# Shared PSUM pools, six split-weight buffers, the sample's attention ahead of the last two prompt tiles, and a new order of emission in a two-layer hybrid encoder

## The chip, the core and the metric

The kernel runs on one NeuronCore of a Trainium2 chip. Its engines are TensorE (PE, with its weight loads as PEld), VectorE (DVE), ScalarE (ACT), GpSimd (POOL) and SyncE (SP, which issues the DMAs). The metric is the device time of one execution in microseconds; lower is better.

## The reference

Two layers over a chunk of 1024 prompt frames and 8 sample streams of 16 frames each, model width 1024, all in float32. Each layer has a mixer (attention over a window of 128 keys with a sink, beside pooling over 2, 4, 8 and 16 frames) and a feed-forward part with a convolution of width 3 and a gate:

```python
def trunk_layer(x, ...):
    xn = rms_norm(x, norm_mix)
    q, k, v, u = mixer_inputs(xn, pos, w_in, q_gain, k_gain)   # one projection, 1024 -> 512+128+128+512
    attn = window_attention_prompt(q, k, v, sinks)             # prompt: 8 q heads, 2 kv heads, chunks of 64
    # sample: keys and values of a cache of 128 positions ahead of the new 16
    pool, new_pool = pool_mixer(u, pool_prev, w_pool, pool_scale)
    x = x + jnp.concatenate([attn, pool], axis=-1) @ w_out
    f, new_conv = conv_ffn(rms_norm(x, norm_ffn), conv_prev, w_up, conv_w, conv_b, w_down)   # D_FF = 2816
    x = x + f
    return x, keys[:, -WINDOW:], vals[:, -WINDOW:], new_pool, new_conv
```

The outputs are both streams' frames, and the newest keys, values, pooling rows and convolution rows.

## The kernel before

**Tiles and numbers.** The 1152 rows (1024 prompt, 128 sample) are nine tiles of 128; tile 8 is the sample. Three tiles make a block b = 0, 1, 2. Float32 products are made from split operands: `hi` is the value rounded by ACT to the fp32r type, `lo` the rest from DVE, and `mm3` makes three matmuls (L173 to L175) of each product.

**The mixer's streams.** Per block there are units k0 to k2 (k, v and q columns; 12 units each), u0 to u2 (pooling input, 8 units), p0 to p2 (the pooling's own matmuls, 4) and o0 to o2 (output projection and the addition to X, 16 units: eight for each half of the columns). n1 to n3 are the norms ahead of a layer's mixer, m0 to m2 those ahead of the feed-forward part. A unit takes one weight piece of 256 KB: SP loads it to `raw`, `w_split` makes hi (ACT, L198) and lo (DVE, L199).

**Attention** is one chain of steps, L.0, L.1 and so on. For a prompt tile: preparation of q and k (`prep`), then for each of two head groups g: `score` (matmuls L606/L607; DVE adds the mask and takes the maximum, L610), `soft1` (exp on ACT, L622), `soft2` (DVE scales, L635), `pt` (transposes of P on TensorE, L645) and `pv` (L658). The next tile's preparation is interleaved. The sample's tile has its own steps (`sample`, among them 64-wide score matmuls per stream, L762/L763), run after tile 7.

**Order.** Every unit and step is a token with a key (a time) and predecessors. The table `PLAN` holds each stream's first key and step (`o0=(87.72, 2.71)`: o0.i has key 87.72 + 2.71 i), the attention's key per tile (`L`), and flags e_*, which put a copy on DVE (1) or ACT (0). `arrange` walks the tokens by key and emits each as soon as its predecessors are out and the counted resources allow; one of these, `mm`, is four PSUM banks: a k or o unit group holds three, a u group two. Tile's scheduler then orders the instructions of each engine anew within their dependences.

**PSUM** is one tile of eight banks, with banks assigned by hand: 0 to 3 from a list (`mm_take`, `mm_give`), 4 and 5 in turn for scores and PV (`s`), 6 and 7 in turn for transposes and the pooling's matmuls (`tr`). The up stage uses banks 0 to 5 as three pairs.

**Feed-forward.** `sums` makes two chains, s0 and s1, for the two halves of the rows, from the transposed norms m: seven roundings (ACT L325, DVE L326) and four sums (L334). Up runs 22 rounds i of seven products n (`PRODUCTS`, a scheme with seven products instead of eight); each unit is 24 matmuls of 288 columns, 12 for each half s. In round 0 the halves are units of their own; the first three of round 0's weights come as `upw` tokens. `up_post` adds the results into rows (L943) or copies them (L949); then follow convolution and gate, stored to `gd` in DRAM. Down runs over three chunks of eight gate blocks, tile by tile: `down_load` reads a tile's gates (SP, then ACT L1055 and DVE L1056), `down_prep` loads and splits one block of down weights (L1044 to L1046). Layer 1's mixer begins under the last down units of layer 0 (tokens d.t).

## Time and profile before

| what | us |
|---|---|
| median of three runs (lowest to highest) | 2417.01 (2414.57 to 2417.25) |
| the profiled execution, its time | 2412.6 |
| its span | 2410.8 |
| TensorE busy | 2280.5 |
| VectorE busy | 1596.4 |
| ScalarE busy | 959.7 |
| mean granted clock of TensorE | 0.969 of full |

Layer 0's mixer takes the span's first 395 us, its up stage the time to 931, its down stage goes to about 1255 with layer 1's first units beside its end; layer 1's up stage runs from about 1605 to 2122. An engine's line in the slices gives its busy share in tenths for each fortieth of the span; PEclk is the clock that TensorE was granted in that slice. A group's row gives the line, engine, operation, what it writes and reads, and its count; then the busy time and the mean ns of one; then the idle time ahead of the group and what ended it. A wait's row gives the waiting line, the line waited for, microseconds in total, times, and the longest. A row of the chain gives start, duration and what.

### The profile page before, as it was taken

To read this page: it belongs to the slowest core of one execution; us is meant where nothing else is said; L and a number is where in the kernel's file an instruction comes from. 1 tells how busy PE (TensorE), PEld (TensorE's weight loads), DVE (VectorE), ACT (ScalarE), POOL (GpSimd) and SP (SyncE) were. 2 spreads that over 40 slices of the span, in tenths; PEclk is the share of its full clock that TensorE was granted. 3 is DMA by queue.
4 is the path that set the end of the run, shared out by engine and by line. 5 is a ranking of instruction groups with operands and counts; after the bars stand their busy time and mean duration, and the time that the engine had idled before them with its cause. 6 is when DMAs were issued, how large, how long until landed. Compare 5 with 4: busy or idle time off the path is not lost.

```text
span 2410.8 us, 35976 instructions
## 1 busy us (share of the span) xinstructions
PE 2280.5 (95%) x13610; PEld 2025.8 (84%) x13610; DVE 1596.4 (66%) x2942; ACT 959.7 (40%) x1774; POOL 201.6 (8%) x411
## 2 busy tenths in 40 slices
PE   7989979899999998999998899788999999989999
PEld 7757757899999997888887687578999999978887
DVE  5766665988888887233356776478888888853332
ACT  4555554534334334121236565454333433421110
POOL 0000000111111110000000000001111111100000
PEclk9989988899999999999999999889999999999999
DMA  6233332222222226364442333422222222273643
GB/s 218 62 112 122 99 117 89 84 79 70 79 75 71 77 75 225 131 218 164 143 135 61 99 127 102 133 89 65 65 80 78 69 79 75 79 246 125 222 157 109
DMA packets 244495, 271.77 MB, mean 113 GB/s; under 512 B 17410, under 2 KB 188370, under 8 KB 244290
## 3 DMA queue, kind: packets, MB, share of 16 engines
q1 hardware_dynamic: 244322, 269.48, 34.9%
q8 instruction: 107, 1.75, 0.3%
q14 instruction: 66, 0.54, 0.1%
HBM read 203.69 MB, written 67.42 MB: 112 GB/s over the span
## 4 chain that ended last, share of the span: by engine, by line
PE 82%; DVE 7%; DMA 5%; ACT 3%; issue 2%; SPq 1%; POOL 0%; ACTq 0%; DVEq 0%
PE psum L173 25%; PE psum L174 25%; PE psum L175 25%; PE psum L658 2%; DMA raw<-in_w_out_dram 2%; DVE W L199 1%; PE psum L305 1%; DVE B L326 1%; DMA raw<-in_w_in_dram 1%; PE psum L645 1%; DMA B<-gd 1%; DMA raw<-in_w_down_dram 1%; DVE B L334 1%; PE psum L461 1%; ACT W L198 1%
## 5 line engine op out<-in xcount | busy, mean ns | idle before, releaser
L173 PE MATMUL psum<-B,W 128*128 128x288 f32 (+1 forms) x1896 | 572.2, 302 | 18.3 <-ACT B L325 12.3
L174 PE MATMUL psum<-B,W 128*128 128x288 f32 (+1 forms) x1896 | 569.9, 301 | 8.1 <-DVE B L326 8.1
L175 PE MATMUL psum<-B,W 128*128 128x288 f32 (+1 forms) x1896 | 568.2, 300 | 0.0
L173 PEld LDWEIGHTS psum<-B,W 128*128 128x128 f32 x1896 | 359.4, 190 | 22.6 <-ACT B L325 13.9
L173 PE MATMUL psum<-B,B 128*128 128x512 f32 (+2 forms) x914 | 357.0, 394 | 20.1 <-ACT B L1055 10.3
L174 PEld LDWEIGHTS psum<-B,W 128*128 128x128 f32 x1896 | 358.8, 189 | 11.2 <-DVE B L326 10.2
L175 PEld LDWEIGHTS psum<-B,W 128*128 128x128 f32 x1896 | 358.9, 189 | 0.9 <-DVE W L199 0.5
L174 PE MATMUL psum<-B,B 128*128 128x512 f32 (+2 forms) x914 | 357.2, 391 | 0.0
L175 PE MATMUL psum<-B,B 128*128 128x512 f32 (+2 forms) x914 | 355.9, 391 | 0.0
L992 DVE SCALAR_TENSOR_TENSOR B<-B,cvp,B 128x1168 f32<-128x1168 f32 x176 | 250.5, 1428 | 7.9 <-ACT B L990 7.7
L173 PEld LDWEIGHTS psum<-B,B 128*128 128x128 f32 x914 | 172.9, 190 | 59.8 <-ACT B L198 11.5
L1083 DVE TENSOR_TENSOR B<-psum,B 128x512 f32<-128x512 f32 x108 | 74.5, 690 | 199.0 <-PE psum L175 198.9
L174 PEld LDWEIGHTS psum<-B,B 128*128 128x128 f32 x914 | 173.5, 190 | 37.6 <-DVE B L199 0.5
L175 PEld LDWEIGHTS psum<-B,B 128*128 128x128 f32 x914 | 172.8, 189 | 37.7 <-issue 0.2
L173 PE MATMUL psum<-W,B 128*128 128x512 f32 (+1 forms) x510 | 190.4, 386 | 9.5 <-ACT B L463 5.0
L199 DVE TENSOR_TENSOR W<-raw,W 128x512 fp32r<-128x512 f32 x184 | 125.8, 689 | 103.4 <-ACT W L198 102.7
L174 PE MATMUL psum<-W,B 128*128 128x512 f32 (+1 forms) x510 | 192.9, 379 | 0.9 <-DVE W L199 0.9
L868 ACT CAST W<-Q 128x512 fp32r<-128x512 f32 x132 | 81.8, 621 | 280.3 <-PE psum L175 280.1
L175 PE MATMUL psum<-W,B 128*128 128x512 f32 (+1 forms) x510 | 191.9, 381 | 0.0
L198 ACT CAST W<-raw 128x512 fp32r<-128x512 f32 x184 | 113.2, 620 | 166.9 <-PE psum L175 58.5
L943 DVE TENSOR_TENSOR B<-psum,PT 128x160 f32<-128x160 f32 (+2 forms) x356 | 147.8, 447 | 27.2 <-PE psum L175 27.1
L943 DVE TENSOR_TENSOR PT<-psum,PT 128x576 f32<-128x576 f32 (+1 forms) x138 | 100.4, 730 | 84.6 <-PE psum L175 84.3
(188 smaller groups left out, 3953.2 us busy)
## 6 DMA issues: line engine op xcount, KB each, us to landing
raw<-in_w_up_dram SPq DMA_DIRECT2D x176, 256.0 KB
xd<-B SPq DMA_DIRECT2D x63, 512.0 KB
B<-xd SPq DMA_DIRECT2D x63, 512.0 KB
raw<-in_w_in_dram SPq DMA_DIRECT2D x120, 256.0 KB
gd<-B SPq DMA_DIRECT2D x44, 576.0 KB
raw<-in_w_down_dram SPq DMA_DIRECT2D x88, 256.0 KB
B<-gd SPq DMA_DIRECT2D x36, 512.0 KB
raw<-in_w_out_dram SPq DMA_DIRECT2D x48, 256.0 KB
```

What stands on the lines that cost most here:

```text
L173: pe.matmul(out=out, lhsT=a[0], rhs=b[0], start=first, stop=False)
L174: pe.matmul(out=out, lhsT=a[0], rhs=b[1], start=False, stop=False)
L175: pe.matmul(out=out, lhsT=a[1], rhs=b[0], start=False, stop=last)
L198: act.copy(out=w.hi, in_=w.raw)
L199: dve.tensor_tensor(out=w.lo, in0=w.raw, in1=f32(w.hi), op=ALU.subtract)
L305: pe.transpose(out=tr[:, k * 128:(k + 1) * 128], in_=xn[:, c:c + 128], identity=ident)
L326: dve.tensor_tensor(out=lo, in0=src, in1=f32(hi), op=ALU.subtract)
L658: pe.matmul(out=o, lhsT=V, rhs=H.pop(("p", g, kk)), start=kk == kks[0], stop=kk == 1)
L868: act.copy(out=hi, in_=src)
L943: dve.tensor_tensor(out=o, in0=x, in1=y, op=ALU.add)
L992: dve.scalar_tensor_tensor(out=c, in0=h[:, j:j + 1168], scalar=cvp[:, j, ct:ct + 1], in1=c, op0=ALU.mult, op1=ALU.add)
L1083: dve.tensor_tensor(out=X[:, hs], in0=o, in1=X[:, hs], op=ALU.add)
```

## The change

- **PSUM**: the one tile with banks assigned by hand becomes pool tiles in rotation: `mm` with four, `s` and `tr` with two each. The pooling's matmuls go from `tr` to `mm`. `arrange` no longer counts `mm`, so groups of all streams may be open together as far as the rotation allows. In the up stage a unit takes a tile of its own for each half.
- **Up's adds**: `up_post` handled both halves with one instruction of 576 columns where it could; now each half has its own (`for s in ss`).
- **Weights**: six W buffers instead of five, 32 B buffers instead of 33; no weights in B buffers any more (`wide`), and a look-ahead of three for all (before, four for some pieces and two for the others).
- **Sample attention**: the tiles go in the order 0 to 5, 8, 6, 7; the preparation of tile 6 is interleaved with the sample's last steps.
- **Gate load**: `down_load(l, 0, 0)` moves from down's first unit into the third unit of up's last round, and the first down weights come one unit later.
- **Keys**: new numbers in `PLAN`, which now also holds those of s0, s1, upw and the d tokens.

```diff
-LA = 4
+LA = 3
...
-    BUFS = dict(B=33, W=5, raw=5, PT=4, Q=4, u=2, sA=1, sB=1, D=2, V=5, st=15, ks=1)
+    BUFS = dict(B=32, W=6, raw=5, PT=4, Q=4, u=2, sA=1, sB=1, D=2, V=5, st=15, ks=1)
...
-    psum = ps.tile([128, 8, 512], F32, name="psum")
-    turn = {"s": [4, 5], "tr": [6, 7]}
-    mmfree = [0, 1, 2, 3]
...
     def P(tag):
-
-        b = turn[tag].pop(0)
-        turn[tag].append(b)
-        return psum[:, b]
+        cnt[0] += 1
+        return ps.tile([128, 512], F32, tag=tag, name=f"{tag}{cnt[0]}", bufs={"mm": 4, "s": 2, "tr": 2}[tag])
...
-        g = T("B" if w.wide else "W", [128, 2, 512], F32R)
+        g = T("W", [128, 2, 512], F32R)
...
-        while upto < len(order) and more < min(order[pos].ahead, order[upto].ahead):
+        while upto < len(order) and more < LA:
...
-            o = P("tr")[:, 0:384]
+            o = P("mm")[:, 0:384]
...
+        seq = (0, 1, 2, 3, 4, 5, 8, 6, 7)
...
-        for t in range(8):
-            first, rest = attend(l, t)
-            if t < 7:
-                nx = [[x] for x in prep_steps(t + 1)]
-            else:
+        for p, t in enumerate(seq):
+            if p + 1 == len(seq):
+                nx = [[] for _ in range(6)]
+            elif seq[p + 1] == 8:
...
+            if t == 8:
+                put(p, sloadv)
+                kc1 = len(out) + 1
+                for i, f in enumerate(srest[:-1]):
+                    put(p, f)
+                    if i >= len(srest) - 7:
+                        more(i - len(srest) + 7)
...
-        pair = (7 * i + n) % 3
         hi, lo = state["upw", 7 * i + n]
         for s in ss:
             ah, al = state["A", s, a]
-            o = psum[:, 2 * pair + s, 0:QT]
+            o = state["upp", s] = P("s" if (7 * i + n) % 3 == 2 else "mm")[:, 0:QT]
...
+        for s in ss:
+            u = state.pop(("upp", s))
+            x = sum_("sum", s)
+            if n == 0:
+                act.copy(out=x, in_=u)
+            elif n == 1:
+                add(hb_first(row(0), s), [u], [x])
...
                     if i == FT - 1:
-                        for x in (2 * n, 2 * n + 1):
-                            if x < CHUNKS[0][1]:
+                        if n == 2:
+                            down_load(l, 0, 0)
+                        for x in (2 * n - 2, 2 * n - 1):
+                            if 0 <= x < CHUNKS[0][1]:
                                 down_prep(l, x)
...
-                if x == 0:
-                    down_load(l, c, t)
...
-                add(f"d.{t}", -44 + t if t < 3 else -30 + 4 * (t - 3), u, [f"d.{t - 1}"] if t else [])
+                add(f"d.{t}", -44 + t if t < 3 else pl["d"][0] + pl["d"][1] * (t - 3), u, [f"d.{t - 1}"] if t else [])
...
-            stream(f"o{b}", ou, pre, {0: {"mm": 3}, 7: {"mm": -3}, 8: {"mm": 3}, 15: {"T6": -6, "mm": -3}})
+            stream(f"o{b}", ou, pre, {15: {"T6": -6}})
...
-                add(f"s{s}.{i}", (246 if s == 0 else 290) + 3 * i, f, pre)
+                add(f"s{s}.{i}", pl[f"s{s}"][0] + pl[f"s{s}"][1] * i, f, pre)
...
-        ev = arrange(toks, {"T6": 18, "qkv": 4, "V": BUFS["V"], "mm": 4})
...
+        ev = arrange(toks, {"T6": 18, "qkv": 4, "V": BUFS["V"]})
```

What the new order does is shown at three places, each in layer 0. A row is a line, an operation, what it writes and what it reads, the shape, and a count where the next rows would be the same; the numbers only tell tiles apart. The changed kernel's lines are 17 to 32 lower.

TensorE at prompt tile 2, from the last score matmuls of head group 1 to the transposes of that group's P. Before:

```order
L606 MATMUL psum_66<-B148_897,Q196_1191 128x256
L607 MATMUL psum_66<-B148_897,Q196_1191 128x256
L645 MATMUL psum_66<-cst_67,B202_1229 128x128 x8
L658 MATMUL psum_66<-PT218_1309,V57_406 128x512
L658 MATMUL psum_66<-PT219_1315,V58_415 128x512
L570 MATMUL psum_66<-cst_67,ks207_1253 128x128 x2
L581 MATMUL psum_66<-cst_67,Q220_1319 128x128 x4
L570 MATMUL psum_66<-cst_67,ks207_1253 128x128 x2
L645 MATMUL psum_66<-cst_67,B210_1262 128x128 x8
```

The changed kernel has 57 split matmuls between the same two points, with other transposes among them; at the end of that stretch, with `mm360` and `mm359` two of o0's open sums:

```order
L149 MATMUL mm360_1665<-W391_1819,B252_1225 128x512
L150 MATMUL mm360_1665<-W391_1819,B252_1225 128x512
L151 MATMUL mm360_1665<-W391_1819,B252_1225 128x512
L149 MATMUL mm359_1661<-W395_1840,B196_960 128x512
L149 MATMUL mm360_1665<-W395_1840,B252_1225 128x512
L150 MATMUL mm359_1661<-W395_1840,B196_960 128x512
L151 MATMUL mm359_1661<-W395_1840,B196_960 128x512
L150 MATMUL mm360_1665<-W395_1840,B252_1225 128x512
L151 MATMUL mm360_1665<-W395_1840,B252_1225 128x512
L618 MATMUL tr303_1438<-cst_66,B276_1324 128x128 x4
L618 MATMUL tr305_1445<-cst_66,B276_1324 128x128 x4
```

The last score matmul of before is followed by transposes of group 0's P (the first L645 row), two PV matmuls (L658), transposes of the next tile's k and q (L570, L581), and then at once by group 1's P (the second L645 row); in the changed order units of u1 and o0 were moved in between, and L618 takes the place of L645.

TensorE at the sample's attention, where its caches are transposed (L751, in the changed kernel L726) and its scores made (L762 and L763, then L737 and L738). Before:

```order
L174 MATMUL psum_66<-W572_3522,B476_2868 128x512
L751 MATMUL psum_66<-cst_67,B526_3174 16x128 x4
L751 MATMUL psum_66<-cst_67,B526_3174 128x128 x4
L175 MATMUL psum_66<-W572_3522,B478_2870 128x512 x3
L751 MATMUL psum_66<-cst_67,B526_3174 128x128 x4
L762 MATMUL psum_66<-B548_3323,B494_2958 64x64
L751 MATMUL psum_66<-cst_67,B526_3174 16x128 x4
```

In the changed kernel:

```order
L150 MATMUL mm735_3474<-W740_3501,B379_1763 128x512
L151 MATMUL mm735_3474<-W740_3501,B379_1763 128x512
L543 MATMUL tr617_2917<-cst_66,ks572_2701 128x128 x4
L737 MATMUL s629_2986<-B608_2883,B556_2631 64x64
L554 MATMUL tr618_2924<-cst_66,Q586_2805 128x128 x4
L738 MATMUL s629_2986<-B609_2884,B560_2662 64x64
```

The 512-wide matmuls around it were o2's, the mixer's last unit group; they are now o1's (L150, L151), and tile 6's transposes of k and q (L543, L554) stand among the scores.

VectorE at the end of the mixer: the last additions to X (L493, L467 in the changed kernel), the chain s0 (L326 and L334, now L302 and L310), up's weights (L851 and L869, now L834 and L852) and a norm (L269, now L245). Before:

```order
L334 TENSOR_TENSOR B525_3172<-B525_3172,B524_3166 128x1152
L199 TENSOR_TENSOR W621_3826<-raw610_3761,W621_3826 128x512
L326 TENSOR_TENSOR B597_3656<-B524_3166,B596_3655 128x1152
L869 TENSOR_TENSOR u654_4005<-raw616_3804,u653_4004 128x512
L326 TENSOR_TENSOR B599_3660<-B537_3244,B598_3659 128x1152
L851 TENSOR_TENSOR Q622_3847<-raw616_3804,raw617_3806 128x512
L326 TENSOR_TENSOR B607_3708<-B525_3172,B606_3707 128x1152
L493 TENSOR_TENSOR B573_3525<-psum_66,B573_3525 128x512
L493 TENSOR_TENSOR B574_3527<-psum_66,B574_3527 128x512
L493 TENSOR_TENSOR B575_3529<-psum_66,B575_3529 128x512
L851 TENSOR_TENSOR Q623_3849<-Q622_3847,raw614_3800 128x512
L851 TENSOR_TENSOR Q624_3851<-raw617_3806,raw614_3800 128x512
```

In the changed kernel:

```order
L852 TENSOR_TENSOR W887_4222<-Q873_4169,W887_4222 128x512
L467 TENSOR_TENSOR B770_3639<-mm824_3953,B770_3639 128x512
L834 TENSOR_TENSOR Q913_4398<-raw903_4350,Q911_4394 128x512
L467 TENSOR_TENSOR B771_3641<-mm825_3957,B771_3641 128x512
L467 TENSOR_TENSOR B772_3643<-mm826_3961,B772_3643 128x512
L852 TENSOR_TENSOR W906_4356<-raw902_4348,W906_4356 128x512
L243 TENSOR_SCALAR st815_3908<-st815_3908 128x1
L245 SCALAR_TENSOR_TENSOR B814_3907<-B604_2869,st815_3908,B650_3113 128x1024
L302 TENSOR_TENSOR B821_3944<-B693_3294,B820_3943 128x1152
L302 TENSOR_TENSOR B828_3966<-B695_3301,B827_3965 128x1152
L302 TENSOR_TENSOR B831_3982<-B715_3382,B830_3981 128x1152
L310 TENSOR_TENSOR B715_3382<-B713_3374,B715_3382 128x1152
```

The chain s0 ended ahead of the last additions to X, with weight steps behind them; the weight steps now stand ahead of the additions, and all of the chain, with the last norm that it needs, behind them.

More of the change, by code (lines that the diff above doesn't have):

```diff
@@ L31, in __init__ @@
     def __init__(self, load, n=512, split=True):
-        self.load, self.n, self.split, self.wide, self.ahead, self.dve = load, n, split, False, 2, False
+        self.load, self.n, self.split, self.dve = load, n, split, False
 class Unit:
@@ L354, in f @@
                         if j == 0:
-                            hold[tl] = mm_take()
-                        o = psum[:, hold[tl], 0:n]
+                            hold[tl] = P("mm")
+                        o = hold[tl][:, 0:n]
                         for kk in range(kn):
@@ L482, in f @@
                         if j == 0:
-                            hold[tl] = mm_take()
-                        o = psum[:, hold[tl]]
+                            hold[tl] = P("mm")
+                        o = hold[tl]
                         if k >= 4:
@@ L943, in add @@
                 dve.tensor_tensor(out=o, in0=x, in1=y, op=ALU.add)
-        uf, us = rows_first(u, ss), rows_second(u, ss)
-        x = sum_("sum")
-        xf = rows_first(x, ss)
-        if n == 0:
-            for o, y in zip(xf, uf):
-                act.copy(out=o, in_=y)
-        elif n == 1:
-            add(hb_first(row(0), ss), uf, xf)
-        elif n == 2:
-            add(xf, uf, xf)
-        elif n == 3:
-            add(rows_first(sum_("tot"), ss), uf, xf)
-        elif n == 4:
-            add(xf, uf, xf)
-            add(hb_second(row(1), ss), us, rows_second(sum_("tot"), ss))
-        elif n == 5:
-            add(hb_first(row(1), ss), uf, rows_first(sum_("tot"), ss))
-            if last:
-                state.pop(("tot", i))
-                frame(i, 1)
-                conv(l, i, 1)
-        elif n == 6:
-            add(hb_second(row(0), ss), us, rows_second(x, ss))
-            if last:
-                state.pop(("sum", i))
-                frame(i, 0)
-                later(1, lambda: gate(l, i))
+        for s in ss:
[5 more added lines that the diff above has]
+                add(hb_first(row(0), s), [u], [x])
+            elif n == 2:
+                add([x], [u], [x])
+            elif n == 3:
+                add([sum_("tot", s)], [u], [x])
+            elif n == 4:
+                add([x], [u], [x])
+                add(hb_second(row(1), s), cut_second(u, s), cut_second(sum_("tot", s), s))
+            elif n == 5:
+                add(hb_first(row(1), s), [u], [sum_("tot", s)])
+            elif n == 6:
+                add(hb_second(row(0), s), cut_second(u, s), cut_second(x, s))
+        if n == 5 and last:
+            state.pop(("tot", i))
+            frame(i, 1)
+            conv(l, i, 1)
+        elif n == 6 and last:
+            state.pop(("sum", i))
+            frame(i, 0)
+            later(1, lambda: gate(l, i))
     def frame(i, val):
@@ L1254, in encoder_kernel @@
                 pre = ([f"s{s}.{i - 1}"] if i else []) + ([ready[i]] if i in ready else [])
[L1255 removed]
+                add(f"s{s}.{i}", pl[f"s{s}"][0] + pl[f"s{s}"][1] * i, f, pre)
         for i in range(3):
[L1257 to L1263 removed]
+            add(f"upw{i}", pl["upw"][0] + pl["upw"][1] * i, lambda l=l, i=i: up_advance(l, i), ["o2.10"])
+        ev = arrange(toks, {"T6": 18, "qkv": 4, "V": BUFS["V"]})
         for t in ev:
```

102 lines of the change are left out of this document (33 added, 69 removed).

## The prediction

> **What bounds the kernel now.** I read the page first: its engine totals, the slices and the chain of what ended last.
>
> ```profile
> span 2410.8 us, 35976 instructions
> PE 2280.5 (95%) x13610; PEld 2025.8 (84%) x13610; DVE 1596.4 (66%) x2942; ACT 959.7 (40%) x1774; POOL 201.6 (8%) x411
> PE   7989979899999998999998899788999999989999
> PEclk9989988899999999999999999889999999999999
> PE 82%; DVE 7%; DMA 5%; ACT 3%; issue 2%; SPq 1%; POOL 0%; ACTq 0%; DVEq 0%
> ```
>
> TensorE is the bound: 95% busy, 82% of the chain. The change leaves its matmuls as they are, so only two things can give time back: the gaps in which it waits (2410.8 - 2280.5 = 130 us, start and end included) and the stretches at half clock. Both lie in the slices where the digits drop. I therefore cut the span into the stages that the change touches: width, then busy time and instructions of PE, PEld, DVE, ACT and POOL, then granted clock, DMA share and rate.
>
> ```profile
> core 0: us, PE busy (x) PEld busy (x) DVE busy (x) ACT busy (x) POOL busy (x), PEclk, DMA share, GB/s
> 11.00:100.00 89.00, 82.88 (x458) 72.08 (x457) 62.77 (x165) 44.69 (x109) 7.20 (x7) 0.96 0.43 141
> 108.00:323.00 215.00, 195.81 (x972) 156.53 (x973) 141.43 (x437) 118.91 (x312) 16.16 (x10) 0.94 0.34 106
> 323.00:394.00 71.00, 56.00 (x286) 39.60 (x285) 34.83 (x76) 30.65 (x77) 3.90 (x5) 0.83 0.33 99
> 394.00:456.00 62.00, 48.69 (x282) 42.42 (x281) 55.97 (x72) 35.10 (x57) 6.81 (x9) 0.83 0.33 104
> 456.00:928.00 472.00, 472.00 (x3558) 471.83 (x3557) 405.15 (x594) 191.93 (x253) 66.45 (x168) 1.00 0.25 80
> 928.00:945.00 17.00, 10.61 (x45) 8.53 (x44) 13.30 (x17) 7.08 (x9) 0.77 (x4) 0.80 0.94 305
> 945.00:1255.00 310.00, 310.00 (x1404) 255.16 (x1403) 114.19 (x176) 67.39 (x107) 4.45 (x5) 1.00 0.51 167
> 1255.00:1519.00 264.00, 244.84 (x1278) 196.36 (x1277) 178.24 (x548) 155.22 (x398) 19.81 (x13) 0.97 0.33 102
> 1519.00:1595.00 76.00, 63.42 (x318) 47.02 (x317) 38.16 (x72) 35.09 (x83) 4.29 (x6) 0.84 0.31 93
> 1595.00:1650.00 55.00, 37.92 (x234) 33.44 (x233) 46.62 (x62) 26.33 (x42) 4.05 (x9) 0.78 0.23 74
> 2118.00:2135.00 17.00, 10.83 (x47) 8.91 (x46) 13.89 (x19) 8.39 (x9) 0.77 (x4) 0.80 0.90 291
> ```
>
> Width less PE busy is idle time; width times (1 - PEclk) is time lost to the clock. The up stage (456 to 928) and the down stage (945 to 1255) lose nothing. What can be won stands in four places, layer 0 and layer 1 together:
> - prompt attention (108:323, 1255:1519): idle 19.2 + 19.2, clock 12.9 + 7.9, so 59;
> - sample attention to the mixer's end (323:394, 1519:1595): 15.0 + 12.6 and 12.1 + 12.2, so 52;
> - start of up (394:456, 1595:1650): 13.3 + 17.1 and 10.5 + 12.1, so 53;
> - up to down (928:945, 2118:2135): 6.4 + 6.2 and 3.4 + 3.4, so 19.
>
> That is 183 us in all.
>
> **Prompt attention: -30.** Between the last score matmul of a tile's second head group and the transposes of its P lie max, exp, sum and scaling on DVE and ACT; meanwhile TensorE needs other work. The two tiles with least of it, 2 and 6, are where it stands:
>
> ```profile
> 130.00:137.00 7.00, 2.61 (x12) 1.97 (x12) 6.60 (x29) 4.96 (x19) 1.96 (x1) 0.69 0.53 162
> 286.00:291.00 5.00, 1.95 (x9) 1.31 (x10) 5.00 (x20) 3.14 (x13) 0.00 (x0) 0.86 0.18 61
> 1329.00:1336.00 7.00, 2.61 (x12) 1.96 (x12) 6.93 (x31) 4.96 (x19) 1.96 (x1) 0.62 0.54 177
> 1475.00:1480.00 5.00, 2.35 (x14) 1.46 (x12) 4.30 (x18) 2.85 (x11) 0.23 (x1) 1.00 0.26 80
> PE psum L645 <- DVE B L635: 14.2, 6, 3.7
> ```
>
> In the first of these windows twelve instructions are all that TensorE has; by the order of before, 16 transposes and two PV matmuls stand between score and P in tile 2. In the changed order 57 split matmuls stand there too (12 of u1, 45 of o0). At the down stage's pace, 310 / 1404 = 0.22 us, that is about 12 us of cover. Over both layers I count in the changed order no tile with less than 9.5 us between score and P; of before, tiles 1 with 9.8 us showed no such wait. The chain itself, four max at 420 ns, four exp at 498 and four scalings at 347 with their hand-overs, is under 7 us:
>
> ```profile
> L610 DVE CUSTOM_DVE_ANT_0 B<-psum,cst 128x256 f32<-128x256 f32 x112 | 42.2, 420 | 27.9 <-PE psum L607 27.6
> L622 ACT ACTIVATE B<-B,st 128x256 f32<-128x256 f32 x112 | 55.5, 498 | 9.0 <-DVE st L613 7.8 <-DVE st L631 1.1
> L635 DVE TENSOR_SCALAR B<-B,st 128x256 f32<-128x256 f32 x112 | 32.2, 347 | 0.2
> ```
>
> The four windows hold 24.0 - 9.5 = 14.5 idle and 5.5 of clock, so 20 goes for sure if the cover holds; of the other 39 (late weights, pool matmuls, shorter halvings) I take a quarter. Ends: 0 and 45.
>
> **Sample attention: -25.** Before, it is the last thing in the mixer, a serial chain with only o2 beside it. Now it stands ahead of tiles 6 and 7, with o1 and u2 around it, and tile 7 closes the mixer over o1's end and o2. But its many 64-wide matmuls cost clock even where TensorE never waits:
>
> ```profile
> 362.00:371.50 9.50, 9.15 (x61) 6.54 (x61) 2.73 (x5) 2.38 (x6) 0.00 (x0) 1.00 0.25 64
> 371.50:382.00 10.50, 10.50 (x41) 7.29 (x40) 2.59 (x7) 3.43 (x9) 0.55 (x1) 0.51 0.11 34
> L762 PE MATMUL psum<-B,B 128*64 128x64 f32 x64 | 12.6, 289 | 0.0
> ```
>
> The clock fell to half behind 9.5 us with only 0.35 idle. I keep those 10.5 x 0.49 = 5.1 per layer, so of 52 at most 42 can go, and take 25, since tile 7's own chain now ends the mixer. Ends: 5 and 42. The Trainium skill, "TensorE: Matmul & The Clock Gate" (section "What's actually happening"), has the clock throttled after an idle window of about 3.4 us. The long waits above agree, the 371.5 us row does not; by the rule the cover alone would bring that 5.1 back too, and the sum would be 10 us lower.
>
> **Start of up: 0.** Its unit of work is a DVE chain for each half of the rows: seven roundings (L326) and four differences (L334), 11 x 1.35 = 14.9 us.
>
> ```profile
> L326 DVE TENSOR_TENSOR B<-B,B 128x1152 fp32r<-128x1152 f32 x28 | 37.4, 1352 | 10.6 <-ACT B L325 10.6
> L334 DVE TENSOR_TENSOR B<-B,B 128x1152 f32<-128x1152 f32 x16 | 21.6, 1353 | 0.2
> L269 DVE SCALAR_TENSOR_TENSOR B<-B,st,B 128x1024 f32<-128x1024 f32 x36 | 46.0, 1282 | 13.9 <-POOL st L268 9.0 <-DMA B<-in_norm_ffn_dram 3.3 <-DMA B<-in_norm_mix_dram 1.4
> PE psum L173 <- ACT B L325: 12.3, 4, 5.1
> L199 DVE TENSOR_TENSOR W<-raw,W 128x512 fp32r<-128x512 f32 x184 | 125.8, 689 | 103.4 <-ACT W L198 102.7
> ```
>
> In layer 0 the first half's chain stood ahead of the last X adds; now all of it stands behind them. From the last X add to the end of the second chain DVE had 11 x 1.35, three norms (L269) at 1.28 and 14 weight steps (512 wide, as L199) at 0.69, 28.4 us; now 22 x 1.35, four norms and one weight step, 35.5. That is 7 worse; but the weight steps now run under o2, and all seven units of the first half stand ahead of the second half's, where four did: I take +5. In layer 1 the same count goes from 35 to 32: -5. Ends: -15 and +20.
>
> **Up to down: -13.** The wait is the load of the first gate block, which SP issues behind 21 loads of down weights (by the order), when the down stage is due:
>
> ```profile
> 930.72 5.14 DMA B<-gd
> 935.88 1.05 ACT B L1055
> PE psum L173 <- ACT B L1055: 10.3, 2, 5.5
> ```
>
> Now it is written into the last round's third unit and stands behind five of them. Four units of 24 matmuls follow it (24 x 472 / 3558 = 3.2 us each, so 13 us), which hide its 6.2 us of load and rounding. The other 11 half blocks of the first down weights wait behind it on SP and come one unit later; they are split on ACT and DVE in a stage where DMA is 94% busy. So 10.3 of wait and some 5 of clock go, and 2 come back. Ends: 0 and 19.
>
> **Up stage: 0.** Five of each round's adds and copies over both halves become two apiece.
>
> ```profile
> L943 DVE TENSOR_TENSOR PT<-psum,PT 128x576 f32<-128x576 f32 x126 | 95.4, 757 | 84.6 <-PE psum L175 84.3
> L943 DVE TENSOR_TENSOR B<-psum,PT 128x576 f32<-128x576 f32 x84 | 63.2, 752 | 14.0 <-PE psum L175 14.0
> L943 DVE TENSOR_TENSOR B<-psum,PT 128x288 f32<-128x288 f32 x96 | 43.3, 453 | 12.8 <-PE psum L175 12.7
> L949 ACT COPY PT<-psum 128x576 f32<-128x576 f32 x42 | 26.9, 640 | 32.7 <-PE psum L175 32.7
> ```
>
> (126 + 84) / 42 = 5 adds a round, 2 x 453 - 755 = 0.15 us each, so 0.75 us. A round of seven units is 22.3 us with 19.1 us of DVE; 19.9 still leaves 2.4. The one copy, on ACT (41% busy there), costs less than its 640 again. TensorE covers both; if that cover were gone, each us over it would cost 44.
>
> W with six buffers, the narrower look-ahead and the mixer's first 108 us: the keys of the units there move both ways; the window in which that could show, 11:100, holds 6 us of idle and 4 of clock. I take 0, ends -5 and +8.
>
> **The sum.** -30 - 25 + 0 - 13 = -68. The new order is sure to bring waits that its rows can't show: of the 59 lost in prompt attention before, 39 lay outside the four worst places; I charge a quarter, 10. So -58: 2410.8 becomes 2353. The profiled execution took 2412.6, below all three runs shown (median 2417.0, 2414.6 to 2417.3); against that median I take 2357.
>
> **The rivals.**
> - The start of up eats the gain (0.15): the first half's chain, no longer under o2, is exposed in both layers, 2 x 14.9 = 30, and the longer gap halves the clock for another 3 a layer; against -58, with its 0 replaced by +36, 2393 against the median. For it: DVE is 56 of 62 us busy there. Against it: layer 1's chain got shorter.
> - The waits only change places (0.12): tile 7 stands where the sample stood, other units wait for the shared banks, and only the load's 13 is sure: 2404.
> - Slower (0.10): the split adds make DVE the bound in the up stage. Price: 44 us for each us by which a round outgrows 22.3. It decides from 58 / 44 = 1.3 us over, that is 3.7 more than the 0.75 counted: waits of DVE on ACT within a round would have to make it. At 2 us over, 88 - 58 = +30, 2447. Against it: in 456:928 TensorE never waits and DVE rests 67 us.
> - No change (0.05): gains and new waits cancel, 2417.
> - The clock follows idle time alone (0.13, faster): by the rule above the sample's 10 come back and halvings shorter than a window vanish: 2345.
> - My forecast, about 2340 to 2380 (0.45).
>
> A difference under 0.2% (4.8 us) can't be told here. Faster: 0.45 + 0.13 + 0.15 + 0.10 of the second rival = 0.83; its other 0.02 lie about no change, so the same 0.06 and slower 0.11. The range leaves out the slower cases and the deepest gains: 2326 (all upper ends but half) to 2408 (only the load pays).
>
> **What will show it.** Right: in the windows about tiles 2 and 6 TensorE is busy and the wait of the P transposes on the scaling (L635 before) is under 4 us in all; the small matmuls of the sample stand among 512-wide ones; the wait for the gate block's rounding is gone; the up stage is 22.2 us a round at clock 1.00. Wrong: an idle stretch of over 20 us at the start of up, waits of matmuls on bank-emptying copies in the mixer, or DVE over 95% in the up stage.

## The result and the profile after

The changed kernel takes 2342.28 us (median of four runs, 2339.62 to 2342.97) against 2415.79 (four runs, 2413.74 to 2417.25): a ratio of 0.9694 with an interval of 0.9677 to 0.9711, 73.5 us less. The prediction said 2357, between 2326 and 2408. The profiled execution took 2341.91 us, its span is 2340.1, and TensorE's mean granted clock 0.984 (0.969 before).

One thing in the text ahead is misnamed. In the sample's attention L727 (now L702) is the score matmul; L751 (L726) transposes its P (its caches are transposed at L692, now L667), and L762 and L763 (L737, L738) are its PV matmuls, over the 128 cache rows and over the 16 new rows. "The sample's 64-wide matmuls" of the prediction are therefore PV.

The page of the changed kernel, its totals and slices:

```profile
span 2340.1 us, 36367 instructions
PE 2253.2 (96%) x13610; PEld 2010.3 (86%) x13610; DVE 1613.6 (69%) x3203; ACT 940.1 (40%) x1765; POOL 186.0 (8%) x411
PE   7989998799999999999999999979999999999999
PEclk9999999899999999999999998989999999999999
```

TensorE waits 2340.1 - 2253.2 = 86.9 us, where it waited 130.3. The dips in both rows of digits are fewer; beside the first slice the deep ones left are the eighth and the 27th, the starts of up in layer 0 and 1. The stages, cut where the prediction cut them (the changed kernel is 20 us ahead at the end of layer 0's up stage):

```profile
core 0: us, PE busy (x) PEld busy (x) DVE busy (x) ACT busy (x) POOL busy (x), PEclk, DMA share, GB/s
11.00:100.00 89.00, 82.76 (x452) 69.97 (x453) 66.44 (x179) 45.03 (x105) 8.11 (x7) 1.00 0.46 150
100.00:384.00 284.00, 268.10 (x1428) 212.74 (x1427) 194.33 (x563) 149.31 (x389) 19.73 (x15) 0.97 0.39 120
384.00:444.00 60.00, 36.48 (x230) 34.23 (x229) 51.09 (x65) 32.53 (x48) 7.17 (x12) 0.80 0.16 52
444.00:916.00 472.00, 472.00 (x3539) 470.73 (x3538) 409.32 (x698) 191.79 (x271) 58.33 (x168) 1.00 0.26 83
908.00:925.00 17.00, 16.63 (x80) 13.43 (x79) 13.52 (x23) 6.69 (x9) 1.91 (x4) 1.00 0.87 260
1236.00:1505.00 269.00, 257.90 (x1390) 207.97 (x1389) 196.63 (x591) 160.63 (x426) 20.01 (x16) 0.97 0.36 110
1505.00:1540.00 35.00, 35.00 (x183) 27.13 (x182) 24.09 (x34) 22.22 (x41) 1.65 (x3) 1.00 0.50 152
1540.00:1580.00 40.00, 27.93 (x160) 25.12 (x160) 35.69 (x42) 19.81 (x31) 5.40 (x7) 0.74 0.20 65
2055.00:2072.00 17.00, 16.02 (x75) 12.77 (x74) 13.78 (x22) 7.74 (x10) 1.91 (x4) 1.00 0.85 260
```

Before these rows are added up, a correction of how the prediction read them. It took width less PE busy as idle and width times (1 - PEclk) as clock loss, and added both. Where TensorE idles at half clock, that counts the same microsecond one and a half times: of the 151.7 us at half clock before, TensorE was idle in 38.1. What the clock costs is half of the busy time inside the half-clock stretches, 113.6 / 2 = 56.8 before and 54.1 / 2 = 27.1 after (the sum over the trace's clock records). With that the account closes: idle -43.4, clock -29.7, TensorE's work at full speed +2.4, in all -70.7, as the spans say. By place, idle and clock loss together:

| place (layer 0 and layer 1) | before | after | change | predicted |
|---|---|---|---|---|
| mixers up to the start of up | 51.7 + 46.4 | 23.9 + 17.5 | -56.7 | -55 + 10 = -45 |
| start of up | 21.0 + 25.8 | 28.6 + 19.8 | +1.6 | 0 |
| up to down | 8.7 + 8.8 | 0.4 + 1.0 | -16.1 | -13 |
| ahead of the mixer's first tile, and the rest | 24.7 | 22.9 | -1.8 | 0 |

The waits of TensorE (line that waits, line waited for; us in total, times, longest):

```profile
PE mm L149 <- DVE B L910: 17.8, 2, 14.8
PE tr L618 <- DVE B L608: 1.2, 2, 0.8
PE mm L435 <- DVE B L438: 3.4, 1, 3.4
PE s L149 <- ACT B L1023: 0.5, 1, 0.5
```

The transposes of P (L645 on L635) waited 14.2 us and now 1.2; the first gate block's rounding (L173 on L1055) cost 10.3 and now 0.5. Those transposes are 13 of the 39 us of idle time that left the mixers (34.2 + 31.8 before, 15.9 + 11.1 now). Two other waits that shrank, before the change:

```profile
PE psum L173 <- ACT B L198: 9.4, 8, 3.4
PE psum L447 <- DVE sA L446: 7.9, 2, 4.4
```

They are split matmuls waiting for the rounding of their weights and transposes of the pooling's outputs; the same waits are 1.5 and 0.6 us now (L149 on L174, L421 on L420). The row of L435 is of another kind: a pooling matmul waits until the step that empties its bank is done. With its likes the waits for one of the four shared banks come to 8.1 us in the mixers, 1.9 before.

The first row is new: split matmuls of up's first round wait for a bank. The chain of layer 0 shows it (start, duration, what):

```profile
414.53 1.37 DVE B L302
415.93 1.37 DVE B L310
...
419.95 1.28 DVE B L310
...
423.80 2.62 DVE B L302 x2
426.42 0.38 DVE B L910
426.84 0.61 PE mm L149
```

```profile
412.00:427.00 15.00, 0.17 (x2) 0.16 (x1) 13.69 (x12) 6.88 (x8) 2.57 (x4) 0.60 0.00 0
```

For 15 us TensorE does nothing. All of the first half's units have run by 407.6, and their results fill the six banks that up may use. The second half's first unit needs one, the bank is given back by an addition (L910) of 0.38 us, and that addition stands in VectorE's queue behind the whole chain s1 (L302 and L310). So s1 holds up first-half results that don't need it. How much of the 14.8 us can be won is another question, since later units of the second half need s1 itself.

### The profile page after: what moved, and what is told of

It is laid out like the page before. It is cut to its first block, busy times and chain, and to the rows that moved or that the text cites. A ratio compares the mean times of both kernels' runs of the same rounds, so it can differ in the third digit from the quotient of the medians.

```text
span 2340.1 us, 36367 instructions
## 1 busy us (share of the span) xinstructions
PE 2253.2 (96%) x13610; PEld 2010.3 (86%) x13610; DVE 1613.6 (69%) x3203; ACT 940.1 (40%) x1765; POOL 186.0 (8%) x411
## 4 chain that ended last, share of the span: by engine, by line
PE 83%; DVE 7%; DMA 5%; ACT 2%; issue 2%; SPq 0%; POOL 0%; DVEq 0%; ACTq 0%
PE mm L149 14%; PE mm L150 14%; PE mm L151 14%; PE s L149 12%; PE s L151 12%; PE s L150 12%; PE s L631 2%; DMA B<-gd 1%; DMA raw<-in_w_in_dram 1%; PE tr L618 1%; DVE B L302 1%; DVE B L310 1%; DVE W L175 1%; DVE B L245 1%; PE tr L554 1%
## 5 line engine op out<-in xcount | busy, mean ns | idle before, releaser
L149 PE MATMUL mm<-B,W 128*128 128x288 f32 (+1 forms) x1376 | 421.2, 306 | 23.7 <-DVE B L910 17.8
L150 PE MATMUL mm<-B,W 128*128 128x288 f32 (+1 forms) x1376 | 415.6, 302 | 1.0 <-DVE B L302 1.0
L151 PE MATMUL mm<-B,W 128*128 128x288 f32 (+1 forms) x1376 | 415.4, 303 | 0.1
L149 PE MATMUL s<-B,B 128*128 128x512 f32 x792 | 312.4, 395 | 1.5 <-DVE B L1049 0.9
L151 PE MATMUL s<-B,B 128*128 128x512 f32 x792 | 312.2, 394 | 0.9 <-DVE B L1024 0.9
L150 PE MATMUL s<-B,B 128*128 128x512 f32 x792 | 312.0, 394 | 0.0
L149 PEld LDWEIGHTS mm<-B,W 128*128 128x128 f32 x1376 | 260.6, 189 | 27.7 <-DVE B L910 18.4
L150 PEld LDWEIGHTS mm<-B,W 128*128 128x128 f32 x1376 | 260.7, 189 | 2.3 <-DVE B L302 1.2
L151 PEld LDWEIGHTS mm<-B,W 128*128 128x128 f32 x1376 | 260.2, 189 | 1.1 <-DVE W L175 0.6
L149 PE MATMUL mm<-W,B 128*128 128x512 f32 (+1 forms) x576 | 213.9, 386 | 8.0 <-ACT B L268 2.8
L150 PE MATMUL mm<-W,B 128*128 128x512 f32 (+1 forms) x576 | 216.6, 377 | 1.5 <-DVE W L175 1.4
L151 PE MATMUL mm<-W,B 128*128 128x512 f32 (+1 forms) x576 | 213.9, 375 | 0.0
L1049 DVE TENSOR_TENSOR B<-s,B 128x512 f32<-128x512 f32 x108 | 74.2, 688 | 175.8 <-PE s L151 175.7
L175 DVE TENSOR_TENSOR W<-raw,W 128x512 fp32r<-128x512 f32 x216 | 145.9, 687 | 65.3 <-ACT W L174 64.5
L851 ACT CAST W<-Q 128x512 fp32r<-128x512 f32 x132 | 81.6, 621 | 261.9 <-PE mm L151 176.2
L149 PEld LDWEIGHTS s<-B,B 128*128 128x128 f32 x792 | 148.7, 188 | 37.6 <-DVE B L1049 1.7
L151 PEld LDWEIGHTS s<-B,B 128*128 128x128 f32 x792 | 148.7, 188 | 36.6 <-DVE B L1024 1.8
L150 PEld LDWEIGHTS s<-B,B 128*128 128x128 f32 x792 | 148.7, 188 | 34.5
L149 PE MATMUL s<-B,W 128*128 128x288 f32 x576 | 172.6, 300 | 1.1 <-ACT B L301 1.1
L150 PE MATMUL s<-B,W 128*128 128x288 f32 x576 | 171.2, 297 | 1.0 <-DVE B L302 1.0
L151 PE MATMUL s<-B,W 128*128 128x288 f32 x576 | 171.1, 297 | 0.0
```

Of the source, the lines that this page charges most:

```text
L149: pe.matmul(out=out, lhsT=a[0], rhs=b[0], start=first, stop=False)
L150: pe.matmul(out=out, lhsT=a[0], rhs=b[1], start=False, stop=False)
L151: pe.matmul(out=out, lhsT=a[1], rhs=b[0], start=False, stop=last)
L175: dve.tensor_tensor(out=w.lo, in0=w.raw, in1=f32(w.hi), op=ALU.subtract)
L851: act.copy(out=hi, in_=src)
L1049: dve.tensor_tensor(out=X[:, hs], in0=o, in1=X[:, hs], op=ALU.add)
```

## The experiments

### The gate load alone, and the split additions alone

To the kernel before: only the earlier load of the first gate block.

```diff
+                        if n == 2:
+                            down_load(l, 0, 0)
-                        for x in (2 * n, 2 * n + 1):
-                            if x < CHUNKS[0][1]:
+                        for x in (2 * n - 2, 2 * n - 1):
+                            if 0 <= x < CHUNKS[0][1]:
                                 down_prep(l, x)
...
-                if x == 0:
-                    down_load(l, c, t)
```

> The kernel before with one part of the change alone: the first gate load in the last up round's third unit, the first down weights one unit later. My theory: this part stands by itself and returns the wait of 5.5 us and the halved clock of 3.4 us in each layer, 18 us as the two windows at the end of up lost 19.4 before and 1.3 after: 2396 to 2402 where before is 2416. Rival (my prediction's term): late weights give some back, 13 us: 2403. Rival: the load was hidden by the rest of the change and alone does nothing: 2412 or more.

Measured: 2398.63 us against 2413.13, ratio 0.9938 (0.9918 to 0.9959), 15 us less (10 to 20 by the interval). The window at the end of up, which read 10.61 busy at clock 0.80:

```profile
928.00:945.00 17.00, 15.42 (x84) 13.28 (x83) 16.28 (x26) 10.17 (x14) 1.17 (x4) 1.00 0.80 255
```

The idle time there falls from 6.4 to 1.6 us and the clock holds (at the end of layer 1's up stage 3.4 us at half clock remain). This term stands by itself.

To the kernel before: one addition or copy for each half of the rows instead of one for both.

```diff
-        elif n == 2:
-            add(xf, uf, xf)
...
+        for s in ss:
+            q = (s,)
+            uf, us = rows_first(u, q), rows_second(u, q)
...
+            elif n == 2:
+                add(xf, uf, xf)
```

> The kernel before with one part alone: the up stage's adds and copies for each half by itself, the bank pairs as before. My theory: DVE has 2.4 us to spare in a round of 22.3, so nothing moves: 2412 to 2420. Rival: DVE becomes the bound in the up stage, 44 us for each us by which a round grows: above 2430.

Measured: 2411.01 us against 2413.13, ratio 0.9997 (0.9981 to 1.0013). The up stage, which read 472.00 with 405.15 of VectorE:

```profile
456.00:928.00 472.00, 472.00 (x3557) 471.83 (x3556) 411.86 (x696) 191.23 (x272) 66.59 (x168) 1.00 0.25 79
```

102 more VectorE instructions and 6.7 us more of its time in the stage, 0.3 us a round where the prediction had 0.75, and TensorE goes on without a gap.

### The sample's place, and the counted banks

The changed kernel with the sample's tile last again:

```diff
-        seq = (0, 1, 2, 3, 4, 5, 8, 6, 7)
+        seq = (0, 1, 2, 3, 4, 5, 6, 7, 8)
```

> The changed kernel with the tiles' attention in the old order, the sample's behind tile 7. My theory: its chain closes the mixer again with only o2 beside it and brings back the prediction's 25 us or more, up to the 42 that its two windows held before: 2367 to 2384 where the changed kernel has 2342. Rival: the cover comes from the open unit groups alone and the sample's place is indifferent: 2339 to 2350.

Measured: 2355.06 us, ratio 0.9757 (0.9735 to 0.9778), between the two expectations: against 0.9694 the place is worth 0.0063 x 2415 = 15 us.

The changed kernel with the four mm banks counted by `arrange`, as before (u0 to u2 too, two each):

```diff
-            kres = {7: {"qkv": 3}, 11: {"V": 3}}
+            kres = {0: {"mm": 3}, 7: {"qkv": 3, "mm": -3}, 8: {"mm": 3}, 11: {"V": 3, "mm": -3}}
...
-            stream(f"o{b}", ou, pre, {15: {"T6": -6}})
+            stream(f"o{b}", ou, pre, {0: {"mm": 3}, 7: {"mm": -3}, 8: {"mm": 3}, 15: {"T6": -6, "mm": -3}})
...
-        ev = arrange(toks, {"T6": 18, "qkv": 4, "V": BUFS["V"]})
+        ev = arrange(toks, {"T6": 18, "qkv": 4, "V": BUFS["V"], "mm": 4})
```

> The changed kernel with the emission again counting four banks for the k, u and o groups, so that a u group and an o group are not open together; keys, sample's place and the rest as changed. My theory: prompt attention loses its cover at some tiles, and 15 to 35 us of its 59 come back: 2357 to 2377. Rival: the new keys make the cover, the shared banks nothing: 2339 to 2348.

Measured: 2370.15 us, ratio 0.982 (0.9797 to 0.9843), 30 us of the gain lost, as the theory had it. The waits of TensorE and the place:

```profile
PE tr L726 <- DVE B L716: 8.8, 2, 8.1
PE tr L618 <- DVE B L608: 3.4, 1, 3.4
264.00:292.00 28.00, 17.75 (x95) 12.20 (x95) 15.62 (x47) 8.51 (x31) 1.95 (x1) 0.64 0.32 101
```

The wait of P's transposes on the scaling of P is back, most of all in the sample's tile: 8.1 us in one piece, with the clock at half behind it.

### Both undone

Both edits above in one kernel.

> The changed kernel with two parts undone at once: the sample's attention behind tile 7 again, and the emission counting four banks for the k, u and o groups. Alone, the first cost 16 us and the second 31 (2355 and 2370 against 2413 for before on the same chip, where the changed kernel's ratio gives 2339). My theory: the two hide different waits and add up: 2339 + 47 = 2386 (2380 to 2392); what is left to the 2398 of the gate load alone, 12 us, is the new keys and buffers. Rival: both hold the same cover, whichever is left is enough for part of it: 2375 or less. Rival: without both, the new keys are worse than the old: above 2395.

Measured, the two edits together: 2367.79 us against 2415.94, ratio 0.9803 (0.9788 to 0.9817). Alone they cost 15 and 30 us, together 26, not 45. The transposes of P in the prompt tiles:

```profile
PE tr L618 <- DVE B L608: 11.5, 3, 5.4
```

The two parts are not two terms. With banks free, the sample's early place gains 15 us; with banks counted, 0.982 and 0.9803 can't be told apart and it gains nothing, and its P's transposes wait 8.1 us there. The reading that fits, not tested further: both draw on the same stock, the units of o1, u2 and o2 that stand between a score and its P; counting keeps some of them closed, and where a tile runs short the wait is at that tile, the sample in one kernel, prompt tiles in the other.

### The old keys with the new structure, and the new keys with the old structure

The changed kernel with the old `PLAN`:

```diff
-    dict(k0=(-31.86, 1.84), u0=(-2.31, 2.93), ..., o0=(92.51, 2.89), ..., o2=(235.82, 3.8), ...
+    dict(k0=(-37.12, 1.06), u0=(-19.58, 1.84), ..., o0=(87.72, 2.71), ..., o2=(244.18, 3.8), ...
+         d=(-30, 4), ..., s0=(246, 3), s1=(290, 3), upw=(286, 6), ...
```

> The changed kernel with the two rows of the old PLAN: shared pools, six W buffers, the sample ahead of the last two tiles and the gate load as changed, only the keys and flags of before (s0, s1, upw and d by the formulas of before). My theory: the structure carries most, the gate load's 15 at least, but keys made for limited banks and another order of tiles open the groups at the wrong time: 2355 to 2385. Rival: the keys are all of it: 2395 or more. Rival: the structure is all of it: 2336 to 2345.

Measured: 2400.17 us against 2415.94, ratio 0.993 (0.9912 to 0.9949). That is what the gate load alone gives (0.9938). Pools, six W buffers, uncounted banks and the sample's place bring nothing more without the keys:

```profile
PE mm L161 <- DVE B L922: 29.7, 2, 14.8
PE tr L738 <- DVE B L728: 9.1, 2, 4.8
108.00:394.00 286.00, 256.72 (x1284) 203.12 (x1284) 177.95 (x509) 150.21 (x387) 19.25 (x15) 0.92 0.35 110
394.00:460.00 66.00, 43.17 (x280) 38.65 (x279) 54.20 (x69) 33.75 (x54) 5.42 (x10) 0.82 0.21 65
```

(Its lines are 12 higher than those of the changed kernel.) The mixer keeps 29.3 us idle, 34.2 before, and both layers have the 14.8 us wait for a bank.

So are the keys all of it? The kernel before with the new keys and nothing else (the same lines the other way round, in the kernel before):

```diff
-                add(f"s{s}.{i}", (246 if s == 0 else 290) + 3 * i, f, pre)
+                add(f"s{s}.{i}", pl[f"s{s}"][0] + pl[f"s{s}"][1] * i, f, pre)
```

> The kernel before with the two new rows of PLAN and the keys that they hold for s0, s1, upw and the d tokens; banks by hand and counted, sample behind tile 7, gate load in the down stage, buffers as before. With all of the change but shared banks and the sample's place the time was 0.9803 of before, the gate load alone 0.9938. Theory: the rest of that, 1.35% or 32 us, is the keys: 0.985 to 0.989, 2377 to 2387. Rival: it is the W buffers, the look-ahead and the pooling's matmuls in other banks: 0.997 or more.

Measured: 2425.60 us (six runs) against 2414.51, ratio 1.0053 (1.0034 to 1.0071). The theory fell; alone the new keys cost 11 us.

```profile
PE psum L633 <- DVE B L623: 15.4, 6, 4.4
```

(Lines 12 lower than those of the kernel before.) P's transposes wait 15.4 us there, 14.2 before, as if the keys had not been changed. That fits the way `arrange` works, where a key only asks for a place and the counted banks decide; which limit refused which unit was not followed.

| | old structure | new structure |
|---|---|---|
| old keys | 1 | 0.993 |
| new keys | 1.0053 | 0.9694 |

The new structure includes the gate load. Neither row nor column holds the gain, only the corner. With banks counted and the sample last 0.9803 is still left of it, 0.0135 or 33 us below the gate load's 0.9938, and the new keys alone don't give that. What remains in that kernel beside the keys and the gate load are the six W buffers and 32 B buffers (no weights among them), the look-ahead of three, the pooling's matmuls in other banks, and PSUM as pool tiles in rotation, in the up stage one for each half (the split additions gave nothing). Which of these carries it was not tried and stays open.

### Layer 1's keys in both layers

In layer 1 the start of up had become shorter (25.8 to 19.8), in layer 0 longer. The keys of the two layers differ there. The changed kernel with the second dictionary of `PLAN` used twice:

```diff
-    dict(k0=(-31.86, 1.84), ..., o2=(235.82, 3.8), ..., m2=(290.7, 1.11), ..., s0=(265.5, 2.44), s1=(284.09, 2.56), ...
+    dict(k0=(-29.58, 0.99), ..., o2=(244.18, 2.25), ..., m2=(282.25, 1.0), ..., s0=(264.1, 4.32), s1=(282.99, 5.86), ...
```

> The changed kernel with layer 1's keys for layer 0 too. In layer 0 the chain s0 stands wholly behind the last X adds, and TensorE loses 23 us idle and 12 of clock at the start of up, in layer 1 with the chain begun under o2 12 and 10. My theory: with layer 1's keys layer 0's start of up loses no more than layer 1's: 10 to 13 us less, 2326 to 2332, unless other places lose by it. Rival: layer 0's loss is not the chain's place but the bank wait behind s1, which stays: 2337 to 2342. Rival: the keys of the other places fit layer 0 worse: above 2345.

Measured: 2325.24 us against 2415.94, ratio 0.9622 (0.9605 to 0.9638); once more, as the base of a later run, 2328.68 against 2413.50, 0.9638 (0.9614 to 0.9662). Both intervals lie below that of the changed kernel (0.9677 to 0.9711).

```profile
PE mm L149 <- DVE B L910: 6.4, 2, 3.4
378.00:433.00 55.00, 41.91 (x266) 39.12 (x265) 49.81 (x66) 27.43 (x44) 8.20 (x11) 0.78 0.21 67
```

The start of up in layer 0 idles 13.1 us instead of 23.5, and the wait for a bank is 3.4 at the longest instead of 14.8. The chain s0 begins ahead of the last additions to X again, so both chains are over sooner. The chain of the profile, once more up to the first addition that empties a bank:

```profile
408.44 3.81 DVE B L302 x3
412.24 0.38 DVE B L910
412.67 0.61 PE mm L149
```

The addition still stands behind s1, but it comes at 412.2 instead of 426.4, 14 us sooner in a span that is 16 us shorter. Not all of that is the chain's place: the last addition to X (L467) already comes 6.5 us sooner, at 379.9 instead of 386.4, for all of layer 0's keys were replaced and not the chain's alone. By idle and clock loss the start of up gains 7 us (28.6 to 21.5), less than the 10 to 13 of the theory. Some 8 us of the 16 are TensorE's work at full speed, which fell from 2226 to 2218 us over the span; why, was not followed, and that the time met the theory is in part luck.

### The banks emptied by ScalarE, ahead of the second chain

A direct test of that wait. In the changed kernel the first half of round 0 is emitted between the steps of the chains, and ScalarE copies each result out of its bank at once; the additions then read the copy.

```diff
+            if i == 0 and s == 0 and n:
...
+                c = state["cp"][:, (n - 1) % 4]
+                act.copy(out=c, in_=u)
+                u = c
...
+        for n, dep in enumerate((0, 1, 7, 4, 8, 10, 2)):
+            add(f"v.{n}", pl["s0"][0] + pl["s0"][1] * dep + 0.1, U[n], ...)
```

> The changed kernel with the results of round 0's first half copied out of their banks by ACT at once, the adds behind them from SBUF, and these units emitted ahead of the chain s1. In the changed kernel TensorE waits 14.8 us for the first of these adds, which stands in DVE's queue behind all of s1. In the order of this one ACT makes the copies behind five of s1's seven roundings. Theory: the banks come free some 5 us earlier and the wait shrinks to 8 to 11, 4 to 7 us less in all: 0.966 to 0.968 of before. Rival: the wait only moves to the chain s1 itself, which these units need: the same time, 0.9694.

Measured: 2332.73 us against 2414.51, ratio 0.9664 (0.9643 to 0.9685), as the theory had it. Against the changed kernel's 0.9694 that is 7 us less, though the two intervals touch; the trace says where from:

```profile
PE mm L149 <- ACT B L918: 10.7, 1, 10.7
380.00:440.00 60.00, 41.38 (x271) 38.98 (x270) 55.06 (x70) 36.99 (x60) 5.77 (x12) 0.86 0.17 53
```

The wait is 10.7 us instead of 14.8, and in the same 60 us the clock is 0.86 instead of 0.80 and TensorE busy 41.4 instead of 36.5. It isn't gone, because ScalarE's queue too has work of the second chain (its roundings, L301) ahead of the copy.

### Which matmuls cost the clock

The prediction kept 5 us a layer for a fall of the clock at the sample's small matmuls, where TensorE hardly waits. After the change the fall is there again, at the same matmuls in another place:

```profile
286.00:292.00 6.00, 5.70 (x43) 3.92 (x41) 1.57 (x4) 2.33 (x5) 0.00 (x0) 1.00 0.31 90
292.00:306.50 14.50, 14.50 (x70) 11.34 (x70) 6.62 (x24) 6.33 (x25) 0.89 (x1) 0.65 0.14 42
```

A kernel of its own, which leaves out the encoder and runs only matmuls on TensorE, in one execution, one stretch for each shape, with 130 matmuls of 128 x 512 ahead of each stretch and nothing to wait for:

```diff
+    for f in (lambda: pv(60), lambda: pv(120, (128,)), lambda: pv(120, (16,)), lambda: score(120), lambda: tr(240), lambda: mix(40)):
+        dense(130)
+        f()
```

> A kernel of its own that computes nothing of the reference: TensorE alone, without a wait, in stretches of 130 fp32r matmuls of 128x128 by 512, and between them 60 pairs of the sample's PV matmul (64 columns of 128 and of 16 rows, 64 wide, float32), 120 of the first kind, 120 of the second, 120 of its score matmul (64 rows, 64 columns, 144 wide), 240 transposes, and 40 times two pairs with two dense ones. Theory from the trace rows: small matmuls halve the clock though TensorE never waits: granted clock about 0.5 in the PV stretches and 1.0 in the dense ones. Rival, the rule that only idle time halves it: 1.0 in all stretches.

Measured, in order of time: pairs of a 128-row and a 16-row matmul of 64 columns as in PV (first row, and after the clock has fallen the second), 128-row alone, 16-row alone, scores over 64 rows, transposes, and last two such pairs in turn with two 128 x 512:

```profile
36.70:40.50 3.80, 3.80 (x32) 2.82 (x30) 0.00 (x0) 0.00 (x0) 1.00 0.00 0
42.00:82.00 40.00, 40.00 (x200) 28.38 (x199) 0.00 (x0) 0.00 (x0) 0.50 0.00 1
115.00:129.00 14.00, 14.00 (x241) 14.00 (x240) 0.00 (x0) 0.00 (x0) 1.00 0.01 2
164.00:180.00 16.00, 16.00 (x153) 16.00 (x152) 0.00 (x0) 0.00 (x0) 0.50 0.00 1
212.00:241.00 29.00, 29.00 (x237) 29.00 (x238) 0.00 (x0) 0.00 (x0) 1.00 0.00 1
272.00:297.00 25.00, 25.00 (x232) 25.00 (x231) 0.00 (x0) 0.00 (x0) 1.00 0.00 1
327.00:393.00 66.00, 66.00 (x393) 41.15 (x394) 0.00 (x0) 0.00 (x0) 1.00 0.00 1
```

In every row TensorE is busy all the time. The clock halves in the two stretches of 16-row matmuls, some 4 us after they begin, and in no other: 64 columns alone don't do it, nor scores, nor transposes. Mixed with 512-wide ones the same pairs run at full clock. So the prediction was right that this loss isn't idle time, and blamed the wrong dimension: it is the 16 contraction rows (L738), not the 64 columns. Heights between 16 and 64 rows were not tried. The Trainium skill, "TensorE: Matmul & The Clock Gate" (section "What's actually happening"), ties the throttle to an idle window; here the clock is 0.50 for 40 us without one, so the rule doesn't cover this case. Why few rows do it, no run shows.

The rows show a second price. Each matmul leaves two records, so a pair is four: 3.80 / 8 = 0.475 us at full clock, while two 128-row matmuls take 2 x 14.0 / 120.5 = 0.232. The 16-row matmuls alone, before their clock falls, are no slower (64 records in the 3.5 us from 159.5 on, 0.109 us a matmul). So it is turning from 128 rows to 16 and back that costs 0.24 us a pair.

### Sixteen rows padded to 128

The base is the kernel with layer 1's keys in both layers (2328.68 us):

> The changed kernel with layer 1's keys in both layers, once more, as the base for the next run: 0.9622 of before, 2318 to 2330.

On it, the sample's second PV matmul runs over 128 rows; the 112 rows beyond the new ones are zeros that GpSimd writes:

```diff
-            H["nv"] = T("B", [16, 8, 128])
+            H["nv"] = T("B", [128, 8, 128])
+            H["pn"] = T("B", [128, 8, 128])
+            pool.memset(H["nv"], 0.0)
+            pool.memset(H["pn"], 0.0)
...
-                        out=H[nm][:, 4 * i:4 * i + 4], ...
+                        out=H[nm][0:n, 4 * i:4 * i + 4], ...
```

> The same with the sample's second PV matmul (L738) made over 128 rows instead of 16, the rows behind zeroed by GpSimd. In the kernel of its own the clock fell to half only in the two stretches with 16-row matmuls, 4 us after their start, and stayed at 1.00 beside 64-column ones of 128 rows. Theory: the 16-row matmuls halve it here too, so the halving of 6.8 us at the sample's PV (288.9 and 1442.6) goes in both layers: 3.4 us each, 7 in all, less 0 to 2 for the zeroing: 0.9593 to 0.9602 of before, 5 to 7 us less than the base. Rival: it is the 64-wide output or the many short matmuls in general: no difference to the base.

Measured: 2308.49 us (2306.66 to 2310.36) against 2413.50, ratio 0.9562 (0.9545 to 0.9579): 20 us less than its base by the medians (18 by the ratios and by the spans) for eight times the rows, some three times what was expected. The base around its PV matmuls:

```profile
281.00:292.50 11.50, 11.50 (x67) 8.71 (x66) 3.84 (x9) 4.08 (x8) 0.00 (x0) 0.66 0.54 188
292.50:302.00 9.50, 9.50 (x36) 6.70 (x36) 3.59 (x13) 2.51 (x11) 0.00 (x0) 0.52 0.15 46
```

and the padded kernel:

```profile
281.00:286.50 5.50, 4.91 (x83) 4.12 (x81) 2.63 (x5) 3.50 (x8) 0.00 (x0) 1.00 0.93 320
1423.30:1429.00 5.70, 4.39 (x81) 3.79 (x80) 2.06 (x3) 4.37 (x9) 0.00 (x0) 1.00 0.57 169
```

In the base the clock falls within the PV matmuls, at 284.6, and is back at 301.6, 5.3 us behind the last of them (296.3), with TensorE busy throughout; padded, it holds 1.00. Of the 18.2 us between the two spans 12.7 are clock, 7.8 TensorE's work at full clock (32 pairs in both layers at 0.24 us are 7.7), and idle time is 2.3 longer. The expectation had no pace, and its 6.8 us at half clock in each layer came from the earlier execution of the same kernel (2325.24 us); in this one the stretches at the PV matmuls are 17.0 and 10.2 us long. How long the clock stays down there differs from one execution to the next. This is the fastest kernel of the case (0.9562 against the change's 0.9694).

## Why the prediction came out

The sign was right and the time lies in the range, which is 82 us wide and also holds the times of three rivals (2345, 2393, 2404); so the hit alone decides little, and the rows must. The sum was 13 us short (-58 against -71 by span), nearly all of it, 12, in the mixers.

- **Up to down, -13.** Measured -16 by the windows and -15 alone. The cover of four units and the price of the halved clock were as counted; the 2 us that were to come back for the later weights can't be told from noise (10 to 20 us alone).
- **Up stage, 0.** Measured 0: 472 us, TensorE never idle, with VectorE up 4 us in the changed kernel and 7 in the kernel with that part alone. The rival that VectorE becomes the bound is out.
- **Prompt attention -30, sample -25, new waits +10.** Measured -57 together. The mechanism it named is real: matmuls now stand between score and P, and P's transposes wait 1.2 us instead of 14.2. But that is a third of the 39 us of idle time won there; the rest lies at waits that the prediction only put among "the other 39", of which it took a quarter (roundings of weights, the pooling's transposes). The new waits that it charged 10 for did come: 8.1 us for shared banks, where 1.9 were before, one of its own signs of being wrong. Two things in the working were not right. The two places were priced as independent, while undoing their parts costs 15 and 30 us alone and 26 together. And the losses themselves were overstated by counting idle time at half clock one and a half times: the two places held 98 us, not 111, and 57 of them came back, where 45 were taken. The share taken was too small and the losses too large, so the two errors partly cancelled.
- **Start of up, 0.** Measured +1.6, as +7.6 in layer 0 and -6.0 in layer 1, where +5 and -5 were taken; the sizes are near. The step that failed is the cover in layer 0: "all seven units of the first half stand ahead of the second half's". They do and they run, but then the banks are full, and what empties them stands behind the second chain. The prediction looked at what TensorE needs as input and not at where its results go. The rival that this start would eat the gain named the right place and the wrong cause: 14.8 of the 21.0 us idle between the last addition to X and the freed bank are s1, through the banks, and only in layer 0; the first half's chain has at most the other 6.
- **W buffers, narrower look-ahead, first 108 us, 0.** Measured -3.2 in the window that the prediction watched (11:100, idle and clock 9.5 to 6.2). That doesn't make them worthless: without the new structure the new keys are 11 us slower, and 33 us of the gain need the keys together with these buffers, the look-ahead, the pooling's banks or the pool tiles. The term was judged by its own window instead of by what it lets others do.
- **The clock at the sample's matmuls, 5 a layer kept.** Right in kind: it moved with the sample to 292 to 306 us. The sign "the small matmuls of the sample stand among 512-wide ones" did not come true: from 286.8 to 301.9 us only transposes and score matmuls stand among them. By the rule that the clock follows idle time alone it would have gone, so that rival was out for its own reason, although its 2345 lies near the result.

## What to carry to other kernels

An order and the resources that allow it have to be judged together: neither the keys nor the buffers and banks were worth anything alone here, and undoing one part at a time gives prices that don't add up when two parts feed the same cover. When TensorE waits for a bank, look at what stands ahead of the emptying instruction in its own queue; there a 0.4 us addition behind a 15 us chain kept TensorE waiting for 14.8 us. And keep matmuls with few contraction rows out of long rows of their own, by zeros up to the full height, or by large matmuls between them (which only the kernel of its own shows).

## What the runs showed of the chip that was not expected

- Float32 matmuls over 16 rows, one after another, halve TensorE's clock though the profile shows it never idle: 0.50 over the 40 us and the 16 us of the two rows, from some 4 us after their start; 128 rows of the same 64 columns keep 1.00.
- A float32 pair over 128 and 16 rows takes 0.475 us at full clock, two over 128 rows 0.232: beside a tall matmul the short one is dearer than a second tall one.
- Half clock outlasts its cause: behind the 16-row matmuls it held for 5.3 us in the base of the padded kernel, and in the kernel of its own for 5.8 us (82.6 to 88.4) and 3.1 us (180.8 to 183.9) of 128 x 512 matmuls without a gap.
